# MLP up-projection: a third pair per quarter as seven block products, and first weight sums by accumulating DMAs

## The chip, the core and the metric

The kernel runs on one core of a Trainium2 chip. The metric is device time in microseconds of one execution, the median of several runs; smaller is better. Five engines work side by side, each through its own list of instructions in order: TensorE (matmuls, "PE" in the profile, its weight loads "PEld"), VectorE ("DVE"), ScalarE ("ACT"), GpSimd ("POOL") and SyncE ("SP", which here only issues DMAs). They wait for one another through semaphores.

## The reference, cut to what matters

Two layers of a hybrid encoder on a 512 x 1024 input: an input projection feeding three branches (a gated linear recurrence, a spatial-gating MLP, a windowed attention), a gated merge, and then the MLP that this change touches:

```
hn = rms_norm(x, ln2[l])
x = x + jnp.square(jax.nn.relu(hn @ w_up[l])) @ w_down[l]
```

`w_up` is 1024 x 4096, `w_down` 4096 x 1024. All data are float32, and the output must be close to a float32 result.

## The kernel before, in words

**Precision.** Each float32 operand is split in a high part (cast to float32r by ScalarE) and a low part (operand minus high part, by VectorE). A product is three matmuls: high x high, high x low, low x high. `wsplit` (L201 to L205) does this for a 128 x 1024 weight chunk: cast L203 on ScalarE into `wh`, subtract L204 on VectorE into `wl`. There are three buffers each of `wh` and `wl` (`WB = 3`). A 512 KB chunk comes from DRAM by one DMA into a `wr` buffer (`WR = 2`) or a `wq` buffer (`NQ = 8`).

**Seven block products.** A 2 x 2 block product needs eight block products in the plain way. `seven` (L422) and `up_pair` (L493) use a Strassen-type scheme with seven: sums of weight blocks and sums of data blocks are formed on VectorE first, and the seven results are added up in PSUM banks and by a few more VectorE and ScalarE operations. `seven` serves the input projection in three units per layer (`"un"`, tiles `t...` and `g...`) and the down projection (`"dn"`, tiles `dA`, `dB`, `dC`). Its four weight blocks are `raw = b11, t3, b22, b21`, two 128 x 1024 chunks each. `t3` arrives as block b12 and must become b12 + b22 first: that is what `early_sums` (L417) does, with two VectorE additions (L420). Later sums are formed inside `seven`: `b11 += t3` before product 6 (L447), `t3 = b11 - b22` before product 5 (L449), `b21 += b11` before product 4 (L451). The products run in the order 1, 2, 6, 7, 5, 4, 3.

**The MLP.** It goes in four quarters `qd` of 1024 hidden columns (loop at the end of `trunk`). A quarter has an up part, eight tiles `f` of 128 hidden columns, and a down part, one call of `seven` with 7 x 24 matmuls of 512 columns. The up tiles come in four pairs `j`. A plain pair is two calls of `proj` (48 matmuls of 512 columns, tile `up`, L208 to L210; relu and square at L1269 and L1270). A seven-product pair is one `up_pair` (84 matmuls of 256 columns, tile `us`, L522 to L524). Before the change, in quarters 1 to 3, pair 1 (`AHEAD`) has its weights loaded early into `wq`, pair 2 (`PAIRS`) into `wr`, and both are seven-product pairs; pairs 0 and 3, and all of quarter 0, are plain.

`up_pair` takes two raw chunks `r0`, `r1`: a full split of `r0` (w1), half-width sums (L499, L500, L503 into PSUM, L505), a half-width split of the PSUM sum (w2, L258 and L259), and, at product 7, full splits of `r1` and `r0` (w3, w4). Its results are gathered in `u` and `v` by L527 to L543. Then `left_first`, `left_second` and `left_sums` (L360 to L407) turn `u` and `v` of each pair into the split operands `sh` that the down block multiplies.

**PSUM banks.** Tags `m`, `a`, `c`, `s`, two banks each. An up pair uses one `c`, one `m` or `s`, and two `a`; a plain up tile one `m` or `s`; the down block both `c`, both `m` and both `a`.

**The order of work.** The program is written in a Tile framework with `schedule_with_timeline_sim=True`: a planner that simulates the engines decides the order of instructions in each engine's list, by readiness and priority (`hp()` raises the priority, `issue_after` through `behind` ties an instruction to another). On the chip the lists are fixed and each engine runs its own in order.

**Queues.** Weights are loaded on SP's queue. POOL's queue carries the stores and loads of `thd`, `mgd` and `xspill` and issues the rest of its small operations (the `rs` powers) in the same list.

Of the kernel before, what the change touches and what calls it, by code (L numbers as in the profile page):

```python
# [9 lines left out]
AF = mybir.ActivationFunctionType  # L10
ALU = mybir.AluOpType
# [22 lines left out]
def _chunk_keys():  # L34

    res = []
    for l in range(DEPTH):

        res += [(l, "bu", i) for i in range(4)]


        res += [(l, "un", u, q, i) for u in range(3) for q in range(4) for i in range(2)]
        for h in range(NH):
            res += [(l, "f", h, 0), (l, "f", h, 1), (l, "q", h)]
        res += [(l, "ck"), (l, "cv")] + [(l, "cq", j) for j in range(4)]
        for d in range(KT):
            res += [(l, "gz", d)] + [(l, "yb", d // 2)] * (d % 2 == 0)
        res += [(l, "ag", h) for h in range(NH)]
        res += [(l, "y", br, fl, i) for br in (2, 0) for fl in range(2) for i in range(2)]
        res += [(l, "wo", fl, i) for fl in range(2) for i in range(4)]  # L50
        for qd in range(4):
            res += [(l, "up", qd, f) for f in range(8)]
            res += [(l, "dn", qd, q, i) for q in range(4) for i in range(2)]
    return res


CHUNK = {k: i for i, k in enumerate(_chunk_keys())}


def trunk(tc, xT, xt, ws, vec, fnb, bsb, snk, wst, rope, cmask, amask, ident, out):  # L60
    nc = tc.nc
# [24 lines left out]
    HOME = {t: p for p, ts in {"G": ("xs", "zt"), "Y1": ("yh",), "br": ("q", "a", "g", "ch"), "Y2": ("yi", "th"), "mlp": ("h", "xm")}.items() for t in ts}  # L86
    part = {}
    BANKS = {"m": 2, "a": 2, "c": 2, "s": 2}
    PAIRS, AHEAD = ((), (2,), (2,), (2,)), ((), (1,), (1,), (1,))
    GROUPS = (("m", "m", "c", "c"), ("a", "a", "s", "s"))  # L90
    WR, WB, NZ, NSM, NQ = 2, 3, 2, 3, 8

# [2 lines left out]
    def nm(s):  # L95
        ctr[0] += 1
        return f"{s}_{ctr[0]}"
# [89 lines left out]
    def uload(*key):  # L187

        raw = []
        for i in range(8):  # L190
            t = part["wq"].tile([P, CW], F32, tag="wq", bufs=NQ, name=nm("wq"))
            with hp():
                nc.sync.dma_start(t, ws[CHUNK[key + (i // 2, i % 2)]])
            raw.append(t)
        return [raw[2 * q:2 * q + 2] for q in range(4)]

    def whl():
        return (sb.tile([P, CW], F32R, tag="wh", bufs=WB, name=nm("wh")),
                sb.tile([P, CW], F32R, tag="wl", bufs=WB, name=nm("wl")))
# [103 lines left out]
    def norm_sums(n, xrows):  # L303

        ss = SM("ss8", 8)
        for j, x in enumerate(xrows):
            nc.scalar.activation(T("jk", "jk"), x, AF.Square, scale=D ** -0.5, accum_out=ss[:, j:j + 1])
        n.rc = rstd_d(ss, 0, 4)
# [94 lines left out]
    def behind(mark):  # L403

        return tc.issue_after(mark.ins) if mark else contextlib.nullcontext()
# [8 lines left out]
            res.append(h)  # L414
        return res

    def early_sums(raw, mark=None):  # L417
        with behind(mark):
            for b12, b22 in zip(raw[1], raw[2]):
                nc.vector.tensor_tensor(b12, b12, b22, ALU.add)  # L420

    def seven(raw, hs, name, on, order=(1, 2, 6, 7, 5, 4, 3), between=None, apart=False, swap=False):  # L422

# [334 lines left out]
    raw, hi, lo = sb.tile([P, CW], F32, tag="wr", bufs=WR, name=nm("wr")), *whl()  # L758
# [27 lines left out]
    for l in range(DEPTH):  # L786
# [39 lines left out]
        hx = left_x(n1, lambda: T("xs", "xs", F32R))  # L826
        if l == 0:
            raw = unit0
            early_sums(raw)
            norm_sums(n1, x0r)  # L830
            boost[0] = True
        rc = n1.rc
# [60 lines left out]
        for u in range(3):  # L893
            nxt = uload(l, "un", u + 1) if u < 2 else None
            if u == 0:
                if l:
                    seven(raw, hx, "t", on_tok, (1, 7, 6, 2, 5, 4, 3), lambda mark: bu.extend(project_bu()), swap=(u + l) % 2)
                else:
                    seven(raw, hx, "t", on_tok, (1, 2, 6, 7, 5, 4, 3), swap=(u + l) % 2)
            else:  # L900
                seven(raw, hx, "g", on_gate(u - 1), between=None if l or u > 1 else rows_behind, swap=(u + l) % 2)
                if l == 0 and u == 1:
                    with behind(kept[0]):
                        for ts in (vt, bv):
                            for i, t in enumerate(ts):
                                nc.scalar.activation(t, t, AF.Copy, scale=rc[:, i:i + 1])
            if nxt:
                early_sums(nxt)
            raw = nxt
        end("G")  # L910
        end("wq")
# [332 lines left out]
        for qd in range(4):  # L1244
            hs, nh = [], [0]

            def new():
                nh[0] += 1
                return T("jk" if nh[0] == 1 else "rb" if nh[0] == 2 else "h", "sh", F32R)

            def keys(j):
                return [(l, "up", qd, 2 * j + i) for i in range(2)]

            early = {j: pair_load(keys(j), True) for j in AHEAD[qd]}
            for j in range(4):
                if j in PAIRS[qd] or j in early:
                    us = up_pair(*(early.get(j) or pair_load(keys(j), False)), hx, "s" if j % 2 else "m")
                for i in range(2):
                    f = 2 * j + i
                    if j in PAIRS[qd] or j in early:  # L1260
                        u = us[i]
                    else:
                        pt = proj(n2.xs, f'up{qd}', l, "up", qd, f, bank="s" if f % 4 > 1 else "m")
                        u = T("z", "u")
                    if f == 0:
                        raw = uload(l, "dn", qd)
                    with hp():
                        if j not in PAIRS[qd] and j not in early:
                            nc.scalar.activation(u, pt, AF.Relu)  # L1269
                            mark = nc.scalar.activation(u, u, AF.Square)  # L1270
                        if f % 2 == 0:
                            hs.append(left_first(new, u))
                        else:
                            rest = left_second(new, hs[-1], u, f == 7)
                    if f == 3:
                        early_sums(raw, mark)

            def between(mark):
                for part_ in rest:
                    with hp():  # L1280
                        part_(lambda: T("l2", "sh", F32R))

            if qd == 3:
                if last:
                    for fl in range(2):
                        fn_t.append(T("z", "fn"))
                        nc.sync.dma_start(fn_t[fl], bass.AP(tensor=fnb.tensor, offset=fnb.offset + fl * S, ap=[[0, P], [1, S]]))
                else:
                    nxt = uload(l + 1, "un", 0)
            down(qd, raw, hs, xr, r2, nr2, done, between, last)  # L1290
        if not last:
            with hp():
                n1.end()
            raw = nxt
            end("mlp")
            begin("G")
            early_sums(raw)
        xsrc = xspill

    for p in reversed(pools):  # L1300
# [119 lines left out]
```

## Time and profile before

| | us |
|---|---|
| runs of the kernel before | 1645.49 (median of 3; 1645.3 to 1646.45) |
| span of the profiled execution | 1644.4 |
| TensorE, VectorE, ScalarE, GpSimd busy in it | 1631.2, 1358.9, 1012.9, 102.4 |

The profile is of one execution, and its span runs from the first to the last instruction. The profiled execution's time outside the span isn't listed; the median of the runs is 1.1 us above the span. In the rows below, L12 is line 12 of the kernel, a row of a timeline has start, duration, engine, line, operation, output tile `<-` input tiles, shape and count, and in brackets how long the engine stood idle before it and what ended that. In a row of groups, "x28 | 34.2, 1223 | 13.3" is 28 instructions, 34.2 us busy, 1223 ns each, 13.3 us of idle time just before them. Neighbouring instructions of one engine can overlap a little, so the distance between starts is the better measure of throughput.

### The profile page before, as it was taken

The page shows a single profiled execution, that of the slowest core. Times are in us where ns is not written, and L with a number is a line of the kernel's source. Part 1 is how long each engine was busy: PE and PEld are TensorE (multiplying, and loading weights), DVE is VectorE, ACT ScalarE, POOL GpSimd, SP SyncE. Part 2 cuts the span into 40 slices and gives each one's busy share as a digit, 9 for nine tenths or more (in the row PEclk, how much of TensorE's full clock was granted, in tenths as well). Part 3 has the DMA queues.
Part 4 walks back from the last instruction along what each step waited for, and adds up shares of the span by engine and source line. Part 5 has one row for each costly group of instructions (what it writes and reads, how often), then busy time and mean ns, then how long its engine had stood idle before and what let it go on. Part 6 is the DMA issues. An engine that isn't in the chain of part 4 may idle for free. (4 is left out here: it accounts for less than half of the span.)

```text
span 1644.4 us, 24323 instructions
## 1 busy us (share of the span) xinstructions
PE 1631.2 (99%) x9137; PEld 1376.8 (84%) x9137; DVE 1358.9 (83%) x2183; ACT 1012.9 (62%) x1731; POOL 102.4 (6%) x165
## 2 busy tenths in 40 slices
PE   9999999999999999999999999999999999999998
PEld 7788888888888898989888888888887888989896
DVE  7888979677758988898989869887877589898887
ACT  7667567677247564646666555886862464647374
POOL 0012000000300000000010110000003000000001
PEclk9999999999999999999999999999999999999999
DMA  8343222222625333232423432223226343232311
GB/s 309 102 154 125 78 90 73 102 97 85 236 92 190 100 106 103 103 115 91 141 90 125 144 121 78 77 91 105 92 86 232 106 162 117 89 128 77 129 65 52
DMA packets 55590, 191.55 MB, mean 116 GB/s; under 512 B 7376, under 2 KB 7632, under 8 KB 55472
## 3 DMA queue, kind: packets, MB, share of 16 engines
q1 hardware_dynamic: 44352, 154.43, 27.3%
q0 software_dynamic: 10688, 35.00, 5.8%
q8 instruction: 72, 1.18, 0.3%
q10 hardware_dynamic: 432, 0.55, 0.1%
q14 instruction: 46, 0.38, 0.1%
HBM read 173.18 MB, written 16.78 MB: 116 GB/s over the span
## 5 line engine op out<-in xcount | busy, mean ns | idle before, releaser
L203 ACT CAST wh<-wq 128x1024 fp32r<-128x1024 f32 x214 | 225.2, 1053 | 205.1 <-PE dA L434 60.9
L204 DVE TENSOR_TENSOR wl<-wq,wh 128x1024 fp32r<-128x1024 f32 x214 | 260.4, 1221 | 62.8 <-ACT wh L203 60.3
L203 ACT CAST wh<-wr 128x1024 fp32r<-128x1024 f32 x164 | 172.0, 1049 | 155.1 <-PE wo L251 27.5
L204 DVE TENSOR_TENSOR wl<-wr,wh 128x1024 fp32r<-128x1024 f32 x164 | 199.9, 1220 | 61.0 <-ACT wh L203 55.1
L210 PE MATMUL up<-xh,wl 128*128 128x512 f32 x320 | 124.8, 390 | 0.0
L209 PE MATMUL up<-xl,wh 128*128 128x512 f32 x320 | 124.8, 390 | 0.0
L208 PE MATMUL up<-xh,wh 128*128 128x512 f32 x320 | 124.6, 391 | 0.0
L434 PE MATMUL dA<-wh,sh 128*128 128x512 f32 x256 | 99.8, 390 | 0.0
L433 PE MATMUL dA<-wh,sh 128*128 128x512 f32 x256 | 98.5, 390 | 0.0
L435 PE MATMUL dA<-wl,sh 128*128 128x512 f32 x256 | 91.9, 389 | 0.0
L656 DVE TENSOR_TENSOR ex<-ex 128x512 f32<-128x512 f32 x112 | 74.9, 686 | 3.5 <-ACT kt L647 3.2
L208 PEld LDWEIGHTS up<-xh,wh 128*128 128x128 f32 x320 | 60.1, 188 | 12.4
L210 PEld LDWEIGHTS up<-xh,wl 128*128 128x128 f32 x320 | 60.1, 188 | 12.3
L209 PEld LDWEIGHTS up<-xl,wh 128*128 128x128 f32 x320 | 60.1, 188 | 12.2
L644 ACT ACTIVATE qt<-ex 128x512 f32<-128x512 f32 x56 | 37.9, 677 | 33.8 <-DVE ex L656 31.8
L433 PEld LDWEIGHTS dA<-wh,sh 128*128 128x128 f32 x256 | 48.1, 188 | 10.0
L434 PEld LDWEIGHTS dA<-wh,sh 128*128 128x128 f32 x256 | 48.1, 188 | 9.9
L435 PEld LDWEIGHTS dA<-wl,sh 128*128 128x128 f32 x256 | 48.1, 188 | 9.9
L523 PE MATMUL us<-xs,wh 128*128 128x256 f32 x192 | 54.1, 283 | 0.0
L522 PE MATMUL us<-xs,wh 128*128 128x256 f32 x192 | 54.1, 283 | 0.0
L524 PE MATMUL us<-xs,wl 128*128 128x256 f32 x192 | 53.4, 283 | 0.0
L208 PE MATMUL gz<-xh,wh 128*128 128x512 f32 x128 | 50.9, 398 | 0.0
(435 smaller groups left out, 4780.6 us busy)
## 6 DMA issues: line engine op xcount, KB each, us to landing
wr<-in_ws_dram SPq DMA_DIRECT2D x158, 512.0 KB, 3.5
wq<-in_ws_dram SPq DMA_DIRECT2D x124, 512.0 KB, 4.3
thd<-zt POOLq DMA_DIRECT2D x32, 256.0 KB, 2.5
gt<-thd POOLq DMA_DIRECT2D x32, 256.0 KB, 3.9
mgd<-mg POOLq DMA_DIRECT2D x16, 256.0 KB, 2.3
mB<-mgd POOLq DMA_DIRECT2D x16, 256.0 KB, 6.7
x<-in_xT_dram SPq DMA_DIRECT2D x8, 256.0 KB, 7.5
xt<-in_xt_dram SPq DMA_DIRECT2D x8, 256.0 KB, 8.3
```

The lines of the kernel that those rows point to most:

```text
L203: nc.scalar.copy(hi, raw)
L204: nc.vector.tensor_tensor(lo, raw, hi.bitcast(F32), ALU.subtract)
L208: nc.tensor.matmul(pt, whi, xhi, start=first, stop=False)
L209: nc.tensor.matmul(pt, whi, xlo, start=False, stop=False)
L210: nc.tensor.matmul(pt, wlo, xhi, start=False, stop=last)
L433: nc.tensor.matmul(pt, xh[:, t], hi[:, c], start=start and k == 0, stop=False, skip_group_check=True)
L434: nc.tensor.matmul(pt, xl[:, t], hi[:, c], start=False, stop=False, skip_group_check=True)
L435: return nc.tensor.matmul(pt, xh[:, t], lo[:, c], start=False, stop=k == 3, skip_group_check=True)
L522: nc.tensor.matmul(pt, hi[:, c], xh, start=n in (1, 2, 7) and k == 0, stop=False, skip_group_check=True)
L523: nc.tensor.matmul(pt, hi[:, c], xl, start=False, stop=False, skip_group_check=True)
L524: nc.tensor.matmul(pt, lo[:, c], xh, start=False, stop=k == 3, skip_group_check=True)
L656: nc.vector.tensor_tensor(o_ap, o_ap, ap_of(ex, i_, [[istep, 2]] + z), ALU.add)
```

## The change

Three edits:

- `PAIRS` is (2, 3) in quarters 1 to 3: pair 3 becomes a seven-product pair as well, with its weights in `wr`. Pair 0 stays plain.
- `early_sums` no longer adds on VectorE. POOL issues, for each of the two chunks of `t3`, a DMA that reads the chunk of b22 from DRAM once more and adds it into `t3` in SBUF. b22 itself is loaded as before.
- The `mark` that tied the MLP's early sums to an activation goes.

```diff
-    PAIRS, AHEAD = ((), (2,), (2,), (2,)), ((), (1,), (1,), (1,))
+    PAIRS, AHEAD = ((), (2, 3), (2, 3), (2, 3)), ((), (1,), (1,), (1,))
...
-    def early_sums(raw, mark=None):
-        with behind(mark):
-            for b12, b22 in zip(raw[1], raw[2]):
-                nc.vector.tensor_tensor(b12, b12, b22, ALU.add)
+    def early_sums(raw, *key):
+        for i in range(2):
+            nc.gpsimd.dma_start(raw[1][i], ws[CHUNK[key + (2, i)]], accum_op=ALU.add)
...
-            early_sums(raw)
+            early_sums(raw, 0, 'un', 0)
...
-                early_sums(nxt)
+                early_sums(nxt, l, 'un', u + 1)
...
-                            mark = nc.scalar.activation(u, u, AF.Square)
+                            nc.scalar.activation(u, u, AF.Square)
...
-                        early_sums(raw, mark)
+                        early_sums(raw, l, 'dn', qd)
...
-            early_sums(raw)
+            early_sums(raw, l + 1, 'un', 0)
```

`early_sums` is called 14 times, so 28 additions become 28 DMAs: three units of the input projection and four down blocks in each of two layers.

## The prediction

> **What bounds the kernel now.** I read the page's busy shares first, then the matmul timeline of one MLP quarter, then what VectorE does in the same stretch.
>
> ```profile
> span 1644.4 us, 24323 instructions
> PE 1631.2 (99%) x9137; PEld 1376.8 (84%) x9137; DVE 1358.9 (83%) x2183; ACT 1012.9 (62%) x1731; POOL 102.4 (6%) x165
> ```
>
> TensorE is never long without work, so time can only go if matmul time goes and if nothing else stops the matmuls. A busy share says little about lost spacing, so I take starts from the timeline: the first and last of 47 plain up matmuls (512 columns), then the first and the 49th of a run of seven-product matmuls (256 columns).
>
> ```profile
> 1395.70 0.39 PE L209 MATMUL up<-xl,wh 128*128 128x512 f32 x1
> 1406.13 0.39 PE L210 MATMUL up<-xh,wl 128*128 128x512 f32 x1
> ...
> 1417.96 0.28 PE L522 MATMUL us<-xs,wh 128*128 128x256 f32 x1
> 1423.72 0.28 PE L522 MATMUL us<-xh,wh 128*128 128x256 f32 x1
> ```
>
> 10.43 / 46 = 0.2267 us for a large one, 5.76 / 48 = 0.120 us for a small one. A quarter with two plain and two seven-product pairs and a down block of 7 x 24 large matmuls needs 96 x 0.2267 + 168 x 0.120 + 168 x 0.2267 = 80.0 us. The chain that ended last gives the measured period, from one quarter's us matmul to the same one in the next:
>
> ```profile
> 1410.95 0.24 PE us L524 x2
> ...
> 1491.24 0.24 PE us L524 x2
> ```
>
> 80.29 us: only 0.3 us of a quarter is not matmul spacing. Most of it is one place, where pair 3's weights come just too late after pair 2 (starts 0.34 us apart, not 0.227; with the step before it about 0.2 us):
>
> ```profile
> 1425.24 0.50 PE L208 MATMUL up<-xh,wh 128*128 128x512 f32 x1
> 1425.58 0.39 PE L209 MATMUL up<-xl,wh 128*128 128x512 f32 x1
> ```
>
> The second engine is VectorE. By ten-microsecond stretches (columns: length, PE, PEld, DVE, ACT, POOL busy, clock, DMA share, GB/s; the first row is the whole quarter):
>
> ```profile
> 1396.00:1476.30 80.30, 80.30 (x434) 69.84 (x433) 69.07 (x95) 44.30 (x67) 0.00 (x0) 1.00 0.31 104
> 1410.00:1420.00 10.00, 10.00 (x85) 9.97 (x85) 9.22 (x16) 6.56 (x13) 0.00 (x0) 1.00 0.28 100
> 1420.00:1430.00 10.00, 10.00 (x72) 9.30 (x71) 9.31 (x15) 8.88 (x17) 0.00 (x0) 1.00 0.51 173
> 1430.00:1440.00 10.00, 10.00 (x46) 8.29 (x45) 9.12 (x16) 6.86 (x13) 0.00 (x0) 1.00 0.11 39
> 1440.00:1450.00 10.00, 10.00 (x46) 8.29 (x45) 10.00 (x14) 5.78 (x7) 0.00 (x0) 1.00 0.00 0
> ```
>
> Over the quarter it has 11 us to spare, but from pair 2 into the down block it is busy 37.65 of 40 us. That stretch decides the change.
>
> **Part 1: pair 3 as seven products, six times (three quarters, two layers).** TensorE drops 48 large matmuls (48 x 0.2267 = 10.88 us) and gains 84 small ones (84 x 0.120 = 10.08): 0.80 us a quarter, 4.8 in all. The 0.2 us stall at plain pair 3 goes with it, 1.2 in all.
>
> The Trainium skill (TensorE: Matmul & The Clock Gate, "Back-to-back issue gap") gives sustained spacings of about 81 ns at 128 columns and 131 ns at 512, weight loads included. On a straight line between them (an estimate, 98 ns at 256) the 84 small ones would cost 8.2 us and the 48 large ones 6.3, so the change would lose 1.9 us a pair, 11.7 in all. The trace disagrees (227 ns at 512 columns, 120 at 256), and the measured spacings stand.
>
> VectorE's extra work comes from the rows of pair 2, which runs today from the same two buffers (wr) that pair 3 will use:
>
> ```profile
> 1412.78 1.22 DVE L204 TENSOR_TENSOR wl<-wr,wh 128x1024 fp32r<-128x1024 f32 x1
> ...
> 1414.52 0.69 DVE L499 TENSOR_TENSOR wr<-wr,wr 128x512 f32<-128x512 f32 x1
> 1415.12 0.42 DVE L535 TENSOR_TENSOR u<-u,us 128x256 f32<-128x256 f32 x1
> 1415.45 0.69 DVE L500 TENSOR_TENSOR wr<-wr 128x512 f32<-128x512 f32 x1
> 1416.05 0.70 DVE L503 TENSOR_TENSOR t<-wr,wr 128x512 f32<-128x512 f32 x1
> ...
> 1417.85 0.69 DVE L259 TENSOR_TENSOR wl<-t,wh 128x512 fp32r<-128x512 f32 x1 [0.78 <-ACT wh L258]
> ...
> 1419.38 1.22 DVE L204 TENSOR_TENSOR wl<-wr,wh 128x1024 fp32r<-128x1024 f32 x1
> ...
> 1420.86 1.22 DVE L204 TENSOR_TENSOR wl<-wr,wh 128x1024 fp32r<-128x1024 f32 x1
> 1421.99 0.42 DVE L259 TENSOR_TENSOR sh<-u,sh 128x256 fp32r<-128x256 f32 x1
> ```
>
> A plain pair has two full splits (L204). A seven-product pair has three, a half split (L259), four half-width adds (L499, L500, L503, L505) and three quarter-width sums (L529, L535, L537). That is one full, five half and three quarter operations more: 1.22 + 5 x 0.69 + 3 x 0.42 = 5.9 us by durations, or 1.13 + 5 x 0.60 + 3 x 0.33 = 5.1 by the spacing of neighbours, which overlap a little.
>
> In the 40 us stretch VectorE then wants 37.65 + 5.1 to 5.9 = 42.8 to 43.6 us. Two adds in it serve a product much later in the down block and can move out, 2 x 1.13:
>
> ```profile
> 1440.24 1.22 DVE L451 TENSOR_TENSOR wq<-wq,wq 128x1024 f32<-128x1024 f32 x1
> ...
> 1445.71 1.22 DVE L451 TENSOR_TENSOR wq<-wq,wq 128x1024 f32<-128x1024 f32 x1
> ```
>
> That leaves 40.5 to 41.3 for matmul work of 39.2. So the matmuls stop 1.3 to 2.1 us a quarter unless more is put off, and up to 4.4 if the 2.35 us that VectorE now idles here stay idle. The operations of pair 3 that the first 10 us of the down block do not need (two half splits, half of one product's adds and its split) come to about 3.5 us, so zero is the lower end. The two places below say where between 0 and 4.4 it lies.
>
> First place, the weights. Both wr buffers are held until pair 2's last two splits, and pair 3's loads are issued just behind them, as the loads for plain pair 3 are now:
>
> ```profile
> 1420.63 0.33 SPq L184 DMA_DIRECT2D wr<-in_ws_dram  x1
> ```
>
> ```profile
> 1422.10 0.33 SPq L184 DMA_DIRECT2D wr<-in_ws_dram  x1
> ```
>
> ```profile
> 1424.14 1.05 ACT L203 CAST wh<-wr 128x1024 fp32r<-128x1024 f32 x1 [0.77 <-DMA wr<-in_ws_dram]
> 1437.66 1.05 ACT L203 CAST wh<-wq 128x1024 fp32r<-128x1024 f32 x1 [2.04 <-PE up L209]
> ```
>
> The first weights are cast at 1425.19, and pair 2 (with its last twelve matmuls no longer behind up matmuls) ends at about 1425.16 + 12 x 0.12 = 1426.6. Products 1 and 2 can start then. But the fifth product (order 1, 2, 6, 7, 5) needs the last split by 1426.6 + 48 x 0.12 + 0.24 = 1432.6. Pair 2 took from 1412.78 to 1421.99, 9.2 us, from its first split to the end of its last; from 1425.19 that is 1434.4, or 1.8 us late. Pair 2's loads had landed long before, so it could begin early; pair 3 cannot. Its own operations alone (3 x 1.13 + 5 x 0.60 + 0.78 of waiting for the cast = 7.2) would end at 1432.4, in time. Between 0 and 1.8 I take 1.2, nearer the upper row, because the sums of the pair before lie between in every pair of the trace.
>
> ```profile
> L542 ACT ACTIVATE u<-us x12: 366/382/393, 603.8 to 1589.4; 128x256 f32<-128x256 f32 x12
> ```
>
> ```profile
> 1429.74 0.62 ACT L543 ACTIVATE u<-u 128x512 f32<-128x512 f32 x1
> ```
>
> Second place, the start of the down block. Today plain pair 3 stands ahead of it, with its last results in other PSUM banks. After the change the block's first product needs the bank that pair 3's last evacuation reads (L542, behind ACT's queue), and the second half of its weights needs the buffer of pair 3's third split, which is free only when pair 3 ends. The 1437.66 row is that kind of wait: a cast held until a matmul lets go. Its cost lies between nothing (cast at once, 1.05 + 1.22 + about 0.3 of handing over, before the matmul that needs it 2.7 to 3.2 us in) and about 1.1 (ACT takes pair 3's relu and square, 0.38 and 0.62 by the two rows, first). I take 0.5. Queued behind these waits are the sums of pair 3 and the down block's second product, on ACT and VectorE.
>
> Together 1.7 us a quarter, 10.2 in six, inside the 0 to 4.4 of the stretch.
>
> **Part 2: the first weight sums by DMA, 28 times.** VectorE loses 28 adds, and its waits for the loads that these read:
>
> ```profile
> L420 DVE TENSOR_TENSOR wq<-wq,wq 128x1024 f32<-128x1024 f32 x28 | 34.2, 1223 | 13.3 <-DMA wq<-in_ws_dram 13.1
> L435 PE MATMUL tA<-wl,xs 128*128 128x512 f32 x48 | 17.1, 394 | 1.4 <-DVE wl L204 1.3
> L874 POOL DMA_DIRECT2D thd<-zt x32 | 17.5, 547 | 188.5 <-ACT zt L889 179.6 <-ACT zt L883 8.3
> ```
>
> In the MLP these adds ran near the end of the preceding down block, outside the crowded stretch, so their 2.4 us a quarter do not relieve pair 3; I credit nothing. In the input projection the matmuls waited 1.3 us in all on VectorE's splits in one block (second row): the gain there lies between 0 and 1.3. POOL, idle in the quarter (0.00 in the first stretch row), pays about 0.55 us to issue each, as for the thd stores. No row shows an accumulating DMA. Its landing is bounded by the plain 512 KB load and by twice the slowest 256 KB load on POOL's queue:
>
> ```profile
> wr<-in_ws_dram SPq DMA_DIRECT2D x158, 512.0 KB, 3.5
> mB<-mgd POOLq DMA_DIRECT2D x16, 256.0 KB, 6.7
> ...
> 1383.25 1.47 SPq L193 DMA_DIRECT2D wq<-in_ws_dram  x2
> 1430.89 1.22 DVE L447 TENSOR_TENSOR wq<-wq,wq 128x1024 f32<-128x1024 f32 x1
> ```
>
> 3.5 to 13.4 us. In the MLP the base loads are issued at about 1384 and their sum is first read at 1430.89, so even the long end is covered. POOL issues each one only when the plain load has landed, and the thd stores queue behind it in the input projection. The open place is the very first block, where the same reader runs early and VectorE would stand still in it:
>
> ```profile
> 25.18 1.22 DVE L447 TENSOR_TENSOR wq<-wq,wq 128x1024 f32<-128x1024 f32 x1
> ```
>
> Cost between 0 and about 5 us once (half of the long end, the rest covered by the sum's own place in the order), against the possible 1.3 of gain. I take 0: the product that needs it is two products (about 11 us) further on.
>
> **The sum.** On the profiled execution: 1644.4 - 4.8 - 1.2 + 10.2 + 0 = 1648.6. The median of the runs is 1.1 us above the span (1645.49 against 1644.4), so **1649.7 us**.
>
> **The rivals.**
> *The stall is hidden* (not slower, faster instead). The planner already fills such gaps: it runs pair 1's last product inside pair 2, and at 92 to 93% VectorE occupancy loses only 0.3 us a quarter. If it also puts off the 3.5 us above, only TensorE's account counts: -4.8 - 1.2, or 1639.5. It decides once the stall is under 0.45 us a quarter. Against it: nothing can start pair 3's loads earlier while pair 2 holds both buffers.
> *A wash.* Stalls near 1 us a quarter eat the 1.0 that is gained: 1642.2 to 1648.8.
> *The accumulation lands late* in the first block, and the matmuls wait behind VectorE: +5 beside the stalls, about 1655.
> *VectorE binds throughout the stretch*: 2.9 us a quarter, 17.4 - 6 = +11.4, 1656.9. This is the upper end of the forecast's own case.
> *The sums leave VectorE to no effect*: already in the sum, at 0.
> *Small matmuls held up by their weight loads*, so that seven products cost more than they save, as in the estimate above: +11.7 and the stalls. Chance 0: all small matmuls quoted run at 0.120.
>
> **How the numbers follow.** About 0.2%, 3.3 us, is what a measurement tells from no change. Forecast (stalls of more than 1.55 us a quarter): 0.43, its own range 1648.8 to 1656.9. Hidden: 0.24. Wash: 0.28. Late accumulation: 0.05. So faster 0.24, same 0.28, slower 0.48. The range must reach the hidden case: 1639.5 to 1656.9.
>
> **What would show it.** Right: us matmul spacing still 0.120; the period near 81.0 us instead of 80.29; gaps in pair 3 from its third to its fifth product and at the first dA matmuls, ended by VectorE's wl (L204, L259) or a cast that waits for TensorE; VectorE over 95% in the stretch. Wrong: a period of 79.3 to 79.8; gaps elsewhere, above all before L447, which would put the cost on the accumulating DMAs; or a landing over 13.4 us.

## The result, and the profile after

The changed kernel takes 1685.58 us (median of 5; 1682.85 to 1687.07), the kernel before, timed beside it, 1645.3 us (1645.01 to 1646.45). The ratio is 1.0242, 95% interval 1.023 to 1.0255: slower by 40 us, where 4.2 were forecast and 11.4 was the upper end. In the rows of after, line numbers behind `early_sums` are lower by one: L521 to L523 are the us matmuls, L446 the sum of product 6 and L450 that of product 4.

Two lines of the page after, then the same us matmul of three successive quarters from its chain of waits:

```profile
span 1683.4 us, 24921 instructions
...
PE 1647.4 (98%) x9353; PEld 1390.7 (83%) x9353; DVE 1365.2 (81%) x2209; ACT 1029.4 (61%) x1767; POOL 120.6 (7%) x193
```

```profile
1441.15 0.24 PE us L523 x2
...
1525.42 0.24 PE us L523 x2
...
1609.29 0.24 PE us L523 x2
```

The busy shares hardly move and say nothing of 39 us. The period does: (1609.29 - 1441.15) / 2 = 84.07 us, against 80.29 before and 81.0 forecast. I then compared the time of the last matmul of each phase in the two traces. The six changed quarters hold 24.7 us (3.5, 4.6, 4.3, then 4.0, 3.6, 4.7), the first projection block 8.8, the start of layer 1 (from layer 0's last down block to layer 1's MLP) 4.4, the end about 1.

**Pair 3.** TensorE's timeline in quarter 1 of layer 0, from pair 3's last product-2 matmul to the first dB matmul of the down block (start, duration; in brackets the idle time and what ended it):

```profile
621.45 0.28 PE L523 MATMUL us<-xh,wl 128*128 128x256 f32 x1
622.71 0.39 PE L521 MATMUL us<-xs,wh 128*128 128x256 f32 x1 [0.98 <-DVE sh L259]
...
623.66 0.39 PE L521 MATMUL us<-xs,wh 128*128 128x256 f32 x1 [0.44 <-ACT wh L203]
...
624.63 0.38 PE L523 MATMUL us<-xs,wl 128*128 128x256 f32 x1 [0.47 <-DVE wl L259]
...
626.36 0.39 PE L523 MATMUL us<-xs,wl 128*128 128x256 f32 x1 [0.28 <-DVE wl L204]
...
634.72 0.50 PE L432 MATMUL dB<-wh,sh 128*128 128x512 f32 x1 [0.41 <-ACT wh L203]
```

By starts, beyond the plain spacing, the first four waits cost 1.14, 0.60, 0.63 and 0.44 us and the fifth 0.57. The four stand inside pair 3, where the prediction put them; the fifth is at the first dB matmul, one product behind the dA that it named. VectorE in the same place: pair 3's first split, pieces of other pairs' sums, pair 3's last split, and the two sums of product 4:

```profile
617.13 1.23 DVE L204 TENSOR_TENSOR wl<-wr,wh 128x1024 fp32r<-128x1024 f32 x1 [0.39 <-ACT wh L203]
...
618.61 1.28 DVE L259 TENSOR_TENSOR sh<-sf,sh 128x512 fp32r<-128x512 f32 x2
...
627.16 1.22 DVE L204 TENSOR_TENSOR wl<-wr,wh 128x1024 fp32r<-128x1024 f32 x1
...
636.80 1.22 DVE L450 TENSOR_TENSOR wq<-wq,wq 128x1024 f32<-128x1024 f32 x1
...
640.95 1.22 DVE L450 TENSOR_TENSOR wq<-wq,wq 128x1024 f32<-128x1024 f32 x1
```

From first to last split it took 11.2 us (9.2 for pair 2 before). The sums of product 4 are still inside the crowded stretch.

Stretches of after (length, then PE, PEld, DVE, ACT, POOL busy, the granted clock, DMA share, GB/s):

```profile
39.90:43.30 3.40, 3.40 (x8) 2.18 (x7) 2.00 (x3) 3.34 (x10) 0.00 (x0) 0.51 0.04 11
46.70:53.50 6.80, 4.75 (x11) 3.79 (x12) 6.77 (x10) 3.04 (x3) 0.00 (x0) 0.50 0.00 0
602.50:647.50 45.00, 42.35 (x283) 38.12 (x282) 43.23 (x67) 30.26 (x52) 0.00 (x0) 1.00 0.20 67
708.90:712.30 3.40, 3.40 (x18) 3.40 (x18) 3.40 (x6) 2.74 (x4) 0.00 (x0) 0.50 0.31 96
```

The third row is pair 2 to the down block: VectorE is busy 43.23 of 45.00 us, 96%. The other three show a granted clock of about 0.50, which no stretch of before shows until its last 5 us.

**The first block.** The first waits of its products 2 and 6, and the DMA rate of after and of before in 1-us slices from 5 to 45 us:

```profile
38.44 0.50 PE L432 MATMUL tB<-wh,xh 128*128 128x512 f32 x1 [2.19 <-ACT wh L203]
45.48 0.50 PE L432 MATMUL tA<-wh,xs 128*128 128x512 f32 x1 [2.12 <-ACT wh L203]
48.75 1.22 PE L434 MATMUL tA<-wl,xs 128*128 128x512 f32 x2 [2.08 <-DVE wl L204]
```

```profile
GB/s 307 168 352 408 401 406 426 422 426 414 418 422 418 430 418 414 422 414 295 266 274 287 274 262 262 340 406 408 397 406 408 406 404 412 239 27 0 0 0 0
```

```profile
GB/s 274 205 338 373 401 391 422 424 412 418 414 418 426 422 418 422 414 422 426 422 401 389 410 404 408 295 326 350 299 389 237 41 17 0 0 0 0 0 0 0
```

From 23 to 30 us, while the two accumulating DMAs run, the rate falls from some 420 to between 262 and 295 GB/s, and the loads are through 4 us later (the slice with 239 against the one with 237).

### The profile page after: what moved, and what is told of

Its sections match the earlier page's. It is cut to its first block, busy times and chain, and to the rows that moved or that the text cites. A ratio compares the mean times of both kernels' runs of the same rounds, so it can differ in the third digit from the quotient of the medians.

```text
span 1683.4 us, 24921 instructions
## 1 busy us (share of the span) xinstructions
PE 1647.4 (98%) x9353; PEld 1390.7 (83%) x9353; DVE 1365.2 (81%) x2209; ACT 1029.4 (61%) x1767; POOL 120.6 (7%) x193
## 5 line engine op out<-in xcount | busy, mean ns | idle before, releaser
L521 PE MATMUL us<-xs,wh 128*128 128x256 f32 x288 | 84.0, 293 | 8.6 <-DVE sh L259 5.9
L209 PE MATMUL up<-xl,wh 128*128 128x512 f32 x224 | 87.3, 390 | 0.0
L210 PE MATMUL up<-xh,wl 128*128 128x512 f32 x224 | 87.3, 390 | 0.0
L523 PE MATMUL us<-xs,wl 128*128 128x256 f32 x288 | 83.6, 295 | 3.7 <-DVE wl L259 2.8
L208 PE MATMUL up<-xh,wh 128*128 128x512 f32 x224 | 86.5, 389 | 0.0
L522 PE MATMUL us<-xs,wh 128*128 128x256 f32 x288 | 82.9, 289 | 0.0
L521 PEld LDWEIGHTS us<-xs,wh 128*128 128x128 f32 x288 | 56.6, 197 | 11.8 <-ACT wh L258 7.2
L521 PE MATMUL us<-xh,wh 128*128 128x256 f32 x216 | 61.9, 289 | 0.0
L523 PEld LDWEIGHTS us<-xs,wl 128*128 128x128 f32 x288 | 56.7, 199 | 5.9 <-DVE wl L259 4.0
L522 PE MATMUL us<-xl,wh 128*128 128x256 f32 x216 | 60.6, 283 | 0.0
L523 PE MATMUL us<-xh,wl 128*128 128x256 f32 x216 | 58.1, 283 | 0.0
L522 PEld LDWEIGHTS us<-xs,wh 128*128 128x128 f32 x288 | 56.7, 197 | 0.5
```

Source lines behind the costliest of these rows:

```text
L208: nc.tensor.matmul(pt, whi, xhi, start=first, stop=False)
L209: nc.tensor.matmul(pt, whi, xlo, start=False, stop=False)
L210: nc.tensor.matmul(pt, wlo, xhi, start=False, stop=last)
L521: nc.tensor.matmul(pt, hi[:, c], xh, start=n in (1, 2, 7) and k == 0, stop=False, skip_group_check=True)
L522: nc.tensor.matmul(pt, hi[:, c], xl, start=False, stop=False, skip_group_check=True)
L523: nc.tensor.matmul(pt, lo[:, c], xh, start=False, stop=k == 3, skip_group_check=True)
```

## The experiments

The expectations call the runs e1 to e18; the text gives these names in brackets. The edits of e3 and e12 are shown against the kernel after, those of e12 and e13 belong to the DMAs alone (e2), and the others are to the kernel before. A quarter is counted net, as its last matmul moved against before in the profiled execution; with a third seven-product pair gross is 1.0 more (the matmul time and stall that this pair saves).

**The parts by themselves** (pairs alone, e1; DMAs alone, e2; both, with the first block's sums on VectorE, e3).

```diff
-    PAIRS, AHEAD = ((), (2,), (2,), (2,)), ((), (1,), (1,), (1,))
+    PAIRS, AHEAD = ((), (2, 3), (2, 3), (2, 3)), ((), (1,), (1,), (1,))
```

> The kernel before with pair 3 as seven products alone; the first weight sums stay additions on VectorE. Theory A (the two edits add up): the trace of after loses about 4.1 us in each of the six quarters with three seven-product pairs (from the end of one down block to the end of the next, 21.2 - 8.8 = 12.4 in layer 0 and 37.9 - 25.6 = 12.3 in layer 1). If that belongs to pair 3, this kernel takes 1645.3 + 24.7 = 1670 us (1666 to 1674), with the gaps inside pair 3 from its third to its fifth product. Rival B (the DMAs do it): the accumulating DMAs on POOL's queue and their traffic disturb the quarters; then this kernel is near my prediction's sum without them, 1640 to 1650.

> The kernel before with the accumulating DMAs alone; two seven-product pairs a quarter as before. Theory A: the DMAs cost the 8.8 us that after loses in the first projection block of layer 0, and perhaps the 4.3 us at the start of layer 1: 1645.3 + 8.8 to 13.1 = 1654 to 1658.5. Rival B: they cost most of the 39 us, 1675 to 1685.

```diff
-            early_sums(raw, 0, 'un', 0)
+            for b12, b22 in zip(raw[1], raw[2]):
+                nc.vector.tensor_tensor(b12, b12, b22, ALU.add)
```

> The kernel after, but the two sums of the very first block (unit 0 of layer 0) are additions on VectorE as before; the other 26 stay DMAs. Theory A (the first block loses its 8.8 us because two accumulating DMAs share the DMA engines with the loads that the first matmuls wait for): 1685.6 - 8.8 = 1676.8, and the first block is as in the kernel before. Rival C (the first block is late because the planner ordered it differently, not because of the traffic): within 3 us of 1685.6.

Measured: pairs alone 1672.36 us, 1.0165 [1.015, 1.0181]; DMAs alone 1655.88, 1.0067 [1.0051, 1.0084]; changed kernel without the first block's DMAs 1675.54, 1.0181 [1.0166, 1.0196]. Pairs alone cost 3.4, 4.2, 4.3, 4.6, 4.1 and 5.2 us in the six quarters, with waits at the same matmuls; TensorE's timeline in quarter 1:

```profile
614.43 0.39 PE L522 MATMUL us<-xs,wh 128*128 128x256 f32 x1 [0.99 <-DVE sh L259]
...
615.38 0.39 PE L522 MATMUL us<-xs,wh 128*128 128x256 f32 x1 [0.45 <-ACT wh L203]
...
616.35 0.38 PE L524 MATMUL us<-xs,wl 128*128 128x256 f32 x1 [0.47 <-DVE wl L259]
```

DMAs alone lose everything in the first block (it ends 9.0 us late, and the MLP's first quarter ends 8.4 late) and nothing after: 26 further adds taken off VectorE gained nothing there, as forecast. Without the first block's DMAs that loss is gone (the block ends 1.7 early). The parts by themselves, 27.1 and 10.6 us, make 37.7 of the 40.3 of the change; most of the rest stands at the start of layer 1 (under "Not in the prediction").

**Where the third pair stands.** Pairs 1 and 3 (pair 2 plain, e4), then pairs 2 and 3 (pair 1 plain, e8), so two pairs as before:

```diff
+    PAIRS, AHEAD = ((), (3,), (3,), (3,)), ((), (1,), (1,), (1,))
```

> The kernel before with pairs 1 and 3 as seven products in quarters 1 to 3 (pair 2 plain), sums on VectorE: as many matmuls as before, but pair 3 stands at the down block and a plain pair lies between the two. Theory D (VectorE has too much to do when three pairs follow each other): the plain pair gives it time, no gaps in pair 3, 1645 to 1648. Rival E (a seven-product pair just ahead of the down block is what costs, through its weight buffers and PSUM banks): 1 us or more a quarter, 1651 to 1657, gaps at the first dA and dB matmuls.

```diff
+    PAIRS, AHEAD = ((), (2, 3), (2, 3), (2, 3)), ((), (), (), ())
```

> The kernel before with pairs 2 and 3 as seven products (pair 1 plain, nothing loaded ahead): as many matmuls as before, two such pairs in a row, the second one with late loads and at the down block. Theory V (three in a row are too much, two are not): the gaps inside pair 3 are small, about as e4, 1655 to 1660. Theory L: pair 3's loads are as late as in e1, its gaps stay, 1645.3 + 6 x 4.7 = 1673.

Pairs 1 and 3: 1656.35, 1.0068 [1.0053, 1.0083], 1.3 to 1.5 us in four of the quarters (2.0 and 2.6 in each layer's last, 1.7 on average), at the first dB and dC matmuls; TensorE's timeline:

```profile
621.14 0.50 PE L433 MATMUL dB<-wh,sh 128*128 128x512 f32 x1 [0.32 <-ACT wh L203]
...
642.53 0.50 PE L433 MATMUL dC<-wh,sh 128*128 128x512 f32 x1 [0.43 <-ACT wh L203]
```

Nothing is lost inside pair 3 there. So the place ahead of the down block costs 1.7 us a quarter with no more work than before. Pairs 2 and 3: 1665.3, 1.0121 [1.0105, 1.0137], 3.3 a quarter on average, between the two forecasts. By the rows of quarter 1 the late weights add one wait of 0.86 inside pair 3, and the dC wait is longer than with pairs 1 and 3 (1.11 against 0.59).

**Pair 3's weights ahead, and VectorE's work.** Pairs 1, 2, 3 with both extra pairs' weights loaded early into `wq` (e5):

```diff
+    PAIRS, AHEAD = ((), (2,), (2,), (2,)), ((), (1, 3), (1, 3), (1, 3))
```

> As e1 (three seven-product pairs, sums on VectorE), but pair 3's weights are loaded ahead into wq with pair 1's, so that they lie ready; pair 2 keeps wr. Theory L (late loads: pair 3's two chunks are loaded only behind pair 2's last splits): the gaps inside pair 3 (3.2 us a quarter in the trace of e1) mostly go, the ones at the down block (about 1.4 a quarter, from e4) stay: 1645.3 + 6 x (1.4 - 0.8) + 1 = 1650. Theory V (VectorE has more to do than time, and does the sums of the pair before in between): the gaps stay, 1665 or more.

The same with the first weight sums by DMA except in the first block (e10):

> As e5 (pair 3's weights loaded ahead), but all first weight sums except those of the very first block are accumulating DMAs. In e5 the down block's first sums came late and ran on VectorE inside the stretch, 2 x 1.13 us. Theory V: without them 2.3 us a quarter come back, 1676.9 - 14 = 1663 (1658 to 1667). Theory L, if the late sums alone hid the use of the early loads: 1648 to 1655. If neither VectorE's work nor the loads count: within 3 us of 1677.

Pairs 1, 2, 3 (as e1) with the operand sums of pair 2 left out (e6):

```diff
+                        if qd and j == 2:
+                            if f % 2 == 0:
+                                hs.append(hs[1])
-                        if f % 2 == 0:
+                        elif f % 2 == 0:
```

> As e1, but in quarters 1 to 3 the operand sums and splits of pair 2's results are left out (the down block reads pair 1's operands in their place), so that VectorE has about 3.5 us and ScalarE 2.3 us less to do while pair 3 runs; pair 3's own chain is untouched. Theory V: the gaps inside pair 3 mostly go, 1672.4 - 6 x 3 = 1654, and 1650 to 1660 is for it. Theory L: the late chunks set the time whatever VectorE has beside them, 1668 to 1672.

All three together (ahead, DMA sums, pair 2's sums left out, e15):

> Pairs 1, 2, 3 as seven products, pair 3's weights loaded ahead as pair 1's are, first weight sums by DMA except in the first block, and the operand sums of pair 2 left out (the down block reads pair 1's operands in their place). If the stall of 5.0 us a quarter is the sum of three parts, pair 3's late chain (about 1.3), VectorE's amount of work (about 2.2) and pair 3's place just ahead of the down block (about 1.4), only the last is left: 0.4 to 0.6 a quarter net, less 1.8 in the first block: 1645 to 1650. If the parts overlap (leaving the sums out had already freed the chain), nothing more goes than with the sums left out alone, 2.0 a quarter: 1655 to 1659.

Ahead: 1676.92, 1.0191 [1.0175, 1.0207], no better than pairs alone. The waits inside pair 3 are gone, but two early sums moved into the stretch, and pair 2 waits instead. VectorE's rows, then TensorE's:

```profile
595.08 1.22 DVE L420 TENSOR_TENSOR wq<-wq,wq 128x1024 f32<-128x1024 f32 x1
...
598.29 1.22 DVE L420 TENSOR_TENSOR wq<-wq,wq 128x1024 f32<-128x1024 f32 x1
```

```profile
603.10 0.39 PE L522 MATMUL us<-xs,wh 128*128 128x256 f32 x1 [1.25 <-ACT wh L258]
```

With those sums on the DMAs: 1668.93, 1.014 [1.0125, 1.0156], 3.0 us a quarter on average; 8.0 us gained over the run before it, where the VectorE theory wanted 14, and outside both forecasts. So adds taken off VectorE do gain where they lie in the stretch. This run and e3 differ in pair 3's early load alone, and e3 lost 4.1 a quarter: the early load is worth 1.1, a part of it clock (e3 has four stretches at half clock in its quarters, e10 one). Sums of pair 2 left out: 1658.99, 1.0081 [1.0063, 1.0099], 2.2 a quarter on average; over the execution this takes 18.7 us of VectorE's busy time and 10.0 of ScalarE's, 3.1 and 1.7 a quarter, and no run separates the two engines. All three: 1657.74, 1.0074 [1.0061, 1.0087], between 0.6 and 1.1 in five quarters and 2.0 in the last, 1.1 on average; its profiled execution was 2 us faster than its median, and it lost 3.4 us more at the start of layer 1. In total that is the range forecast for parts that overlap (1655 to 1659), and not the 1645 to 1650 of parts that add up; by quarters, 1.1 lies between the two (0.4 to 0.6 and 2.0). The stretch in the last two runs (columns as in the stretches above):

```profile
594.00:637.00 43.00, 41.57 (x277) 37.54 (x277) 39.81 (x58) 28.08 (x48) 0.00 (x0) 1.00 0.19 63
```

```profile
593.90:635.90 42.00, 41.25 (x274) 37.32 (x274) 39.13 (x58) 27.46 (x47) 0.00 (x0) 1.00 0.20 64
```

VectorE is at 93% in both, near the 94% before the change (37.65 of 40 us). What is left in the second stands at the first dA and dB matmuls, the place ahead of the down block:

```profile
614.93 0.50 PE L432 MATMUL dA<-wh,sh 128*128 128x512 f32 x1 [0.29 <-ACT wh L203]
...
621.90 0.50 PE L432 MATMUL dB<-wh,sh 128*128 128x512 f32 x1 [0.32 <-ACT wh L203]
```

Pairs alone lose 4.3 us net a quarter on average, 5.3 gross. Of these, 2.1 go with pair 2's sums (4.3 to 2.2), 1.1 more with the weights ahead and the first sums on the DMAs (2.2 to 1.1), and 2.1 gross are left. In the other order the split is nearly the same: weights ahead and DMA sums alone give back 1.4 (4.3 to 3.0), pair 2's sums then 1.8 (3.0 to 1.1). That the 2.1 that are left belong to the place is read from the waits at dA and dB and from the 1.7 of the run with pairs 1 and 3; no run takes the place away alone.

**Order of the work.** Ordinary priority for the sums of pairs 1 and 2 (e7); the sums of product 4 tied behind product 6, alone (e9) and with the weights ahead and DMA sums (e11):

```diff
+                    with contextlib.nullcontext() if qd and j in (1, 2) else hp():
                         if f % 2 == 0:
```

> As e1, but the operand sums and splits of pairs 1 and 2 go to the planner without the raised priority that everything around them has, so that it may put pair 3's weight splits ahead of them. Theory V with order as the cause (the same work, in a better order, fits): the chain from pair 3's first split to its last gets shorter than the 11.2 us of e1, and the time falls by 1 to 3 us a quarter, 1654 to 1666. If the amount of work decides and not the order: within 3 us of 1672, with the gaps moved to the down block.

```diff
-                        V.tensor_tensor(b21[i], b21[i], b11[i], ALU.add)
+                        with behind(ends[6] if name == "d" else None):
+                            V.tensor_tensor(b21[i], b21[i], b11[i], ALU.add)
```

> As e1, but in the down blocks the two adds for product 4 (b21 += b11, the ones that my prediction let move out of the crowded stretch) may be issued only behind the last matmul of product 6. Theory V (VectorE's work in the stretch sets the time): 2.3 us of work leave the stretch, so up to 2 us a quarter come back, 1672.4 - 12 = 1660 (1656 to 1665), with shorter gaps at the first dB and dC matmuls. Rival P (only the chain inside pair 3 counts, and these adds run after it): 1670 to 1674.

> e9 and e10 together. Theory V: 4.5 us of VectorE's work a quarter leave the stretch of e5, 1676.9 - 6 x 4.3 = 1651 (1647 to 1657); it would have to be under 1645 to beat the kernel before, which needs the stall to be under 0.8 us a quarter. Rival P: no better than e10.

1672.88 (1.0166 [1.015, 1.0182]), 1672.73 (1.0165 [1.0148, 1.0182]) and 1669.99 (1.0144 [1.0129, 1.0159]): no change, and no test either. In the first the planner wrote nearly the same list. In the second the sums ran at 628.36 and 632.50 us, as at 628.53 and 632.68 without the tie, and in the third they stayed as well. Whether moving them out helps is open. Two more buffers for `wr` or `wh` would be the direct way and were not tried.

**The other end of the quarter.** Pairs 0, 1, 2 (e16); the same with pair 2's sums left out (e17); and pairs 0 and 2 alone, as much work as before (e18):

```diff
+    PAIRS, AHEAD = ((), (0, 2), (0, 2), (0, 2)), ((), (1,), (1,), (1,))
```

> Pair 0 instead of pair 3 as the third seven-product pair (weights in wr), pair 3 plain, sums on VectorE as before. Theory place and crowding: pair 0 runs just after the down block, where VectorE stood idle for 4.8 of 10 us, and the plain pair stays ahead of the next down block; the matmul time falls by 0.8 a quarter and little is lost: 1640 to 1643.5. Rival, the late chain: pair 2's weights now wait for pair 0's buffers as pair 3's waited for pair 2's, about 1.3 us a quarter: 1646 to 1650. Rival, the amount: VectorE's 5 us more a quarter come into the stretch from pair 2 to the down block all the same, about 2 us a quarter: 1652 to 1660.

> As the run with pairs 0, 1, 2 as seven products (1665.37, 3.2 us a quarter net, about 4 gross), but the operand sums of pair 2 left out (the down block reads pair 1's operands in their place), which takes some 4 us of VectorE's work out of each quarter. Theory of the amount: VectorE's load falls back below that of the kernel before, and 2 us a quarter or more go: 1645 to 1653. Theory of the place: the stalls are at pair 0's late first weights and at pair 2's, whose buffers pair 0 held, and stay: 1660 to 1666.

```diff
+    PAIRS, AHEAD = ((), (0, 2), (0, 2), (0, 2)), ((), (), (), ())
```

> Pairs 0 and 2 as seven products, both with their weights in wr, pairs 1 and 3 plain: as many seven-product pairs as before, so VectorE has the same amount of work, but no pair's weights are loaded ahead. Theory of the amount: no more work, no more stall, 1644 to 1648. Theory of the place: pair 0's weights (0.9 to 1.3 us late in the run with pairs 0, 1, 2) and pair 2's stand as they stood there: 2 us a quarter, 1655 to 1660.

1665.37 (1.0123 [1.0109, 1.0137]), 1658.91 (1.0083 [1.0069, 1.0097]) and 1654.88 (1.0058 [1.0045, 1.0071]). My hope for pair 0 fell: it costs 3.0 us a quarter net there too, more than any of the three forecasts, and the waits are spread, at pair 0's first weights, pair 2's, plain pair 3's and the down block's:

```profile
581.32 0.38 PE L522 MATMUL us<-xs,wh 128*128 128x256 f32 x1 [0.74 <-ACT wh L203]
...
605.95 0.39 PE L522 MATMUL us<-xh,wh 128*128 128x256 f32 x1 [0.29 <-ACT u L533]
...
609.48 0.50 PE L210 MATMUL up<-xh,wl 128*128 128x512 f32 x1 [0.16 <-DVE wl L204]
...
642.95 0.50 PE L434 MATMUL dC<-wh,sh 128*128 128x512 f32 x1 [0.41 <-DVE sh L259]
```

Less work takes 6.5 us off (0.8 a quarter, the rest at the start of layer 1), between its two forecasts, and pair 0 with no more work than before still costs 9.4 (1.3 a quarter), close to the lower end for the place. In its quarter 2 the largest wait is in pair 0, at product 2, for VectorE's evacuation of the down block's dA bank (L478); that one starts at 660.25, behind a split and three sums of pair 0 itself:

```profile
661.05 0.39 PE L522 MATMUL us<-xh,wh 128*128 128x256 f32 x1 [0.69 <-DVE xr L478]
```

So a seven-product pair next to a down block loses time on either side, and the amount of work comes on top. In this last run both pairs' weights also come through `wr`; how much of the 1.3 is due to that is not shown.

**The first block.** The two DMAs as plain copies (so the traffic without the adding, and that block's sums left out, e12), then the norm sums tied behind product 6, with the DMAs (e13) and in the kernel before (e14):

```diff
-            early_sums(raw, 0, 'un', 0)
+            for i in range(2):
+                nc.gpsimd.dma_start(raw[1][i], ws[CHUNK[(0, 'un', 0, 2, i)]])
```

> As e2 (accumulating DMAs, two seven-product pairs), but in the very first block the two DMAs on POOL's queue are plain copies of the same 512 KB over the same tiles, without the addition (so that block's sums are left out). Theory T (an accumulating DMA uses the DMA engines about twice, as the rate of 262 to 295 GB/s for 6 us in the trace of after suggests): the dip goes, and half or more of the first block's 9 us with it: 1655.9 - 4.5 to 9 = 1647 to 1651. Rival W (the wait for the load and then for the second landing is what costs): the first block loses as much as in e2, 1654 to 1657.

```diff
-            norm_sums(n1, x0r)
...
+                    with behind(bv[-1]):
+                        norm_sums(n1, x0r)
```

> The accumulating DMAs alone (pairs as before), with the eight norm sums of the first projection block (ScalarE, L307) tied behind the first evacuation of product 6, so that product 6's weight casts no longer stand behind them in ScalarE's list. Theory Q (order): in the run with the accumulating DMAs alone 3.8 us of the first block's 9 were the wait for product 6's first cast, which stood behind all eight norm sums, and these waited for loads that landed late; that wait goes and so do most of the 1.7 us waited for xt before it: 1649 to 1651. Theory W (landing): the cast and the sum before it are late because the second DMA lands late, whatever else is in the lists: 1654 to 1656.5.

> Control for the run above: the kernel before with the same eight norm sums tied behind product 6. In the kernel before the first block lost some us as well (VectorE's sums), but no cast of product 6 stood behind all norm sums. Both theories: 1643.5 to 1646.5. Over 1647 would mean that moving the norm sums costs something of its own, to be taken off the reading of the run above.

Plain copies: 1653.72, 1.0049 [1.0034, 1.0064], 7.9 us over before where the accumulating ones took 10.6, though the rate does not dip at all (the two intervals of the ratio overlap; in the profiled executions the block ends 6.2 and 9.0 late); DMA rate as above:

```profile
GB/s 244 195 305 379 389 408 420 424 410 434 418 414 426 410 430 418 414 426 410 430 401 410 434 401 428 404 402 406 404 412 408 364 152 31 0 0 0 0 0 0
```

Norm sums later: 1653.09, 1.0048 [1.0034, 1.0062], also 7.9 over before, between the two forecasts; the control 1643.49, 0.9992 [0.9983, 1.0001], so 1.7 of the 2.7 us gained come without the DMAs, and 1.0 is left for theory Q, less than these intervals resolve. VectorE with the norm sums later, then TensorE:

```profile
34.15 1.23 DVE L204 TENSOR_TENSOR wl<-wq,wh 128x1024 fp32r<-128x1024 f32 x1 [3.16 <-ACT wh L203]
...
40.43 1.22 DVE L446 TENSOR_TENSOR wq<-wq,wq 128x1024 f32<-128x1024 f32 x1
...
43.89 1.22 DVE L446 TENSOR_TENSOR wq<-wq,wq 128x1024 f32<-128x1024 f32 x1
```

```profile
42.83 0.50 PE L432 MATMUL tA<-wh,xs 128*128 128x512 f32 x1 [2.58 <-ACT wh L203]
...
46.30 1.22 PE L434 MATMUL tA<-wl,xs 128*128 128x512 f32 x2 [2.27 <-DVE wl L204]
```

The DMAs were issued at 20.31 and 21.55 us and landed after at most 12.1 us, so by 33.7. The sums that read them run at 40.43 and 43.89, and no bracket says that they waited: they stand there in VectorE's list, though VectorE stood still for 3.16 us at 31 to 34 us. In the kernel before they ran at 25.18 and 30.32. So theory W, that the landing itself holds the sum up, does not fit this trace either. The planner placed the sums just ahead of product 6; the trace shows that order, no run tested it alone.

No version is clearly faster than the kernel before: that kernel with its norm sums later is the fastest, and its interval touches no change.

## Why the prediction was wrong

**Right.** Slower, by stalls at the places named. The us matmuls keep their spacing of 0.120 us: the matmul side of the sum, -6.0 us, stands, and the rival of small matmuls held up by their weight loads does not. With two seven-product pairs the MLP's and the later units' accumulating DMAs are covered, and taking their adds off VectorE gains nothing. That the direction came out right says little: 4.2 us of loss were forecast, and 40 came.

**The step that failed first: the stall term, 1.7 us a quarter, 10.2 in all.** Measured gross it is 24.7 / 6 + 1.0 = 5.1 a quarter, 31 in all. I let the two places stand for everything and used VectorE's account only as bounds, 0 to 4.4. Of the terms:

- "The second place", the start of the down block, was put at 0.5 between 0 and 1.1. The runs give 1.7 (pairs 1 and 3) to 2.1 (what is left when the other two are taken away). I counted one cast; the traces have a wait at two or three of the first dA, dB and dC matmuls.
- "The first place", pair 3's weights, was put at 1.2. Loading them ahead gives back 1.1 (e3 to e10). That size was about right, although the chain took 11.2 us and not the 9.2 of pair 2, because more of the other pairs' sums lie between.
- The amount of work was the missing term: leaving out pair 2's sums, 3.1 us of VectorE's and 1.7 of ScalarE's time, gives back 2.1. I had written that two adds (2.26 us) "can move out" and 3.5 us more be put off. In the trace the adds stayed. An operation that could run later runs later only if the order of the list says so, and the planner's list did not. The 4.4 was therefore no far end: the measured 5.1 lies beyond it. Two of the three costs I had added up; the third, which I used only as a bound on them, comes on top.

**The rival "VectorE binds throughout the stretch"**, 2.9 a quarter, had the right mechanism for a good part of it; its price was too low as well.

**The step that failed second: 0 for the first block, between 0 and 5.** It is 9.0 at the block's end in the run with the DMAs alone and 8.8 in the change. I had priced the landing (forecast 3.5 to 13.4, measured 9.6 median) and let "the sum's own place in the order" cover the rest; that place did not hold, the sum moved from 25.18 to 42.26 us in the change. Some 2 to 3 us belong to the adding (plain copies are that much cheaper). The rest lies between the order of VectorE's and ScalarE's lists, which changed with the DMAs, the second reading of b22 (1.05 MB, about 2.5 us at the plain copies' 410 GB/s, an estimate) and the clock (6.8 us at half clock in e2, e12 and e13, so up to 3.4 us). This split is argued from rows and not shown by a run.

**Not in the prediction.** The start of layer 1 loses 4.4 us. It loses 0.9 with pairs alone and nothing with the DMAs alone, but 3.4 to 6.3 in the four other runs that have pairs 1, 2, 3 and DMA sums (e3, e10, e11, e15). So it belongs to the two edits together. In all five TensorE stands there twice for ScalarE; in the change:

```profile
849.72 0.81 PE L330 MATMUL xT<-id_t,xr 128*128 128x128 f32 x4 [0.88 <-ACT xf L335]
...
851.33 1.34 PE L208 MATMUL bu<-xh,wh 128*128 128x512 f32 x4 [0.80 <-ACT xh L258]
```

The kernel before and the two parts alone don't have these waits. In four of the five a stretch at half clock follows (below), in e15 none. Other pairs without DMA sums lose up to 2.4 there at another wait. Why ScalarE is late only with both edits stays open.

## What to carry to other kernels

An engine at 94% beside one at 99% had little slack here: leaving out 3.1 us of VectorE's and 1.7 of ScalarE's work a quarter gave back 2.1 us of time. Whether work can be put off has to be checked in the order of the list; whether a list written by hand would let it leave the stretch was not shown. Cost the late weights, the amount and the place as terms that add up, and treat the bound from the busy engine as a forecast and not as a far end. A new kind of operation also changes the planner's order around it, so its price is not only its landing; and two edits that are cheap somewhere alone can cost there together.

## What the runs showed of the hardware

**Half the clock after short stalls.** TensorE's timeline in quarter 2 of after, in pair 3:

```profile
705.33 0.28 PE L523 MATMUL us<-xh,wl 128*128 128x256 f32 x1
706.60 0.38 PE L521 MATMUL us<-xs,wh 128*128 128x256 f32 x1 [0.99 <-DVE sh L259]
...
707.54 0.38 PE L521 MATMUL us<-xs,wh 128*128 128x256 f32 x1 [0.44 <-ACT wh L203]
...
708.51 0.39 PE L523 MATMUL us<-xs,wl 128*128 128x256 f32 x1 [0.47 <-DVE wl L259]
...
709.26 0.41 PE L521 MATMUL us<-xs,wh 128*128 128x256 f32 x1
709.47 0.41 PE L522 MATMUL us<-xs,wh 128*128 128x256 f32 x1
```

From 708.9 the same matmuls start 0.21 us apart instead of 0.12, for 3.4 us, with the granted clock at 0.50. The stalls ahead of it are those of quarter 1, which lost no clock. In this trace three of the six quarters have such a stretch, and they lost 4.6, 4.3 and 4.7 us; the three without lost 3.5, 4.0 and 3.6, on average 0.8 less. The first block has 10.2 us at half clock, the start of layer 1 3.4. The Trainium skill (TensorE: Matmul & The Clock Gate, "Part 1: The HAM clock gate (the "warmup" mystery)") has a free-running window of about 3.4 us and half the clock after an idle one. The trace agrees on the length and the grid: 39.9 and 708.9 lie 669.0 us apart, 196 windows of 3.413. But the window before 708.9 was not idle: TensorE was busy 1.51 of its 3.41 us, and by starts the matmuls stood still for about 2.4. On the same grid the windows ahead of the other stretches, the one at the very end left out (39.9, 46.7, 794.2, 852.2, 1627.0), were busy 1.4, 1.3, 2.1, 1.8 and 1.7 us, while two with 2.0 (from 1538.3) and 2.1 (from 620.1, in quarter 1) were followed by full clock. In quarter 1 a border of the grid, at 623.56, cuts the stalls in two. So in this trace short stalls take the clock when they leave less than some 2 us of work in one window; by this measure the border is not sharp.

**An accumulating DMA is slower than a plain one and slows others.** Issue and landing on the page after:

```profile
L419 POOL DMA_DIRECT2D wq<-in_ws_dram x28 | 24.4, 870 | 559.9 <-DMA wq<-in_ws_dram 264.6
...
wq<-in_ws_dram SPq DMA_DIRECT2D x124, 512.0 KB, 4.6
wq<-in_ws_dram POOLq DMA_DIRECT2D x28, 512.0 KB, 9.6
```

It takes 870 ns to issue where a plain copy of the same size on the same queue took 530 (e12), and 9.6 us to land where a plain load on SP's queue takes 4.6. Part of that second difference is the queue and the moment: in the first block the two plain copies of e12 landed after 8.8 us, the two accumulating DMAs of e2 after 10.5. While two of them run, the whole core's rate is down by a third; the plain copies leave it at 401 to 434 GB/s.
